# A decoder trunk's experts: gather from unsplit tokens with a twelfth weight buffer, and the second transposition behind both down products

## Chip, core and metric

The kernel runs on one core of one Trainium2 chip. The metric is the device time of one execution in microseconds; the figures of the runs are medians. Engine names: PE is TensorE (matmuls and transpositions), PEld its weight loads, DVE is VectorE, ACT is ScalarE, POOL is GpSimd, SP is SyncE, which issues the transfers.

## What is computed

A two-layer decoder trunk on 256 tokens of 1024 features, all float32. Each layer is a mixer (layer 0: pooling and sliding-window attention; layer 1: dilated attention and a gated short convolution) and a feed-forward part (layer 0: dense SwiGLU of width 2816; layer 1: eight experts of width 3584, the best two per token), each followed by a LayerNorm of the scaled residual sum. The change lies in the experts:

```
def moe_swiglu(x, w_router, w_gate, w_up, w_down):
    top_logit, top_e = lax.top_k(logits, TOP_K)          # TOP_K 2 of N_EXPERTS 8
    gates = jax.nn.softmax(top_logit, axis=-1)
    ...
        return (jax.nn.silu(xb @ w_gate[e]) * (xb @ w_up[e])) @ w_down[e]
    ...
    out = jnp.zeros((T + 1, d), jnp.float32).at[row_tok].add(y.astype(jnp.float32) * row_gate[:, None])
```

## The kernel before

**Weights.** All weights come from HBM as one long sequence of pieces, 128 partitions by 2048 float32 (1 MB), issued by SP (L191) into raw buffers as these come free. In the experts there are eleven such buffers (two opened at the start, seven in `raws`, and the tiles `xth` and `xtl` lent later). A piece is used as a sum of two single-pass fp32r halves: `W.hi` casts `wh` from the raw piece on ACT (L258), `W.lo` subtracts `wl = raw - wh` on DVE (L275) and gives the raw buffer back. There are four `wh` tiles and three `wl` tiles. `W.drop`, called when a piece has been consumed, issues the next cast and the next subtraction; all instructions stand on each engine in the order in which the Python code issues them (a manual schedule). Some pieces, called native, are not split: a float32 matmul reads the raw piece itself.

**Experts.** One unit per expert. Expert 0 and the two experts with most tokens have units of 128 token slots (heavy); the five others have 64 (light). `Experts.step` does one unit and one chunk of 512 of the 3584 columns: gate (two pieces), up (two pieces), and then the down products (two pieces) of the step before it. In a heavy unit each chunk product is three fp32r matmuls, its down pieces are native in the part where light and heavy alternate (L1224, `acc<-raw,hf`). In a light unit the high and low halves of the tokens stand side by side as 128 columns (`ml`), so a product is two matmuls (L1226 with `wh`, L1227 with `wl`) and the two halves of the result must be added afterwards: ACT copies the bank to `h` (gate L1427, up L1439), PE transposes `h` in four pieces into a bank (L1237), ACT copies one half (L1240) to `sg` (gate) or `us` (up), and DVE adds the other (L1241). Transposition and copy are `fold_of`; the add is the function that it returns. `sg * us` follows on DVE (L1466), then ACT's cast `hh` (L1467), and DVE's remainder (L1468) is left to the next step (`settle`).

**Order of steps.** Expert 0, then mostly light, light, heavy, sometimes light, heavy, and at the end seven steps of light expert 5 alone. A pair below is two light steps in a row; the first stands behind a heavy step, so the down products in it are native, and those in the second are of a light step.

**Gather.** A unit's tokens are gathered by matmuls with a one-hot matrix `oh` (L1179). The tokens were split beforehand into `xk` high and low (ACT L1089 and L1115, DVE L1091 and L1306), so a unit takes 32 fp32r matmuls of 128 rows: four parts for a heavy unit (three copied out of PSUM by ACT, one by DVE, L1185), two for a light one (both by ACT, L1190). The parts are issued between the products of other steps, one each time `part` is called.

Of the kernel before, what the change touches and what calls it, by code (L numbers as in the profile page):

```python
# [10 lines left out]
F32 = mybir.dt.float32  # L11
F32R = mybir.dt.float32r
# [75 lines left out]
def trunk(ctx, tc, stream, x_tok, x_t, pos, ln_w, ln_b, pool_bd, pool_sc, sinks, conv_w, router, cf, cb, windows,  # L88
# [20 lines left out]
    def bank():  # L109
        return rings.next("bank") if "bank" in rings.at else ps1.tile([128, 512], F32, name="bank")  # L110
# [16 lines left out]
    def split(hi, lo, src):  # L127
        nc.scalar.copy(hi, src)
        nc.vector.tensor_sub(lo, src, hi.bitcast(F32))
# [757 lines left out]
    with tc.tile_pool(name="od1", bufs=1) as e1, tc.tile_pool(name="od2", bufs=2) as e2:  # L887
# [151 lines left out]
    identb = cbf[:, B_ID:B_TRI]  # L1039
    early.close()  # L1040
    raw3 = ctx.enter_context(tc.tile_pool(name="raw3", bufs=1))
    xk, yb = [raw2.tile([128, PIECE], F32R, name=f"xk{i}") for i in range(2)], \
        raw2.tile([128, PIECE], F32R, name="yb")
    raws = [raw3.tile([128, PIECE], F32, name=f"raw{RAW1 + i}") for i in range(RAW2 + RAW3 - 3)]
    lasting = raws[:3]
    W.give_back(*raws)
    mm, na, nb, oa, ob = proj_out(wb, lambda: None)
    ctx.enter_context(tc.manual_schedule())
    xkh, xkl = [t.rearrange("p (i d) -> p i d", i=2) for t in xk]
    lgp = bank()  # L1050
    lg0 = lgp[:, :2 * NE].rearrange("p (i e) -> p i e", e=NE)

    def route(norm, c):
# [8 lines left out]
            for k in range(2):  # L1062
                nc.tensor.matmul(lg0[:, i], xt[:, k], rw[:, c + k], start=c + k == 0, stop=c + k == KC - 1)
        return logits

    def split_tokens(i):
        split(xkh[:, i], xkl[:, i], x[:, i])

    na.add(1, oa[1])
    na.finish()  # L1070
# [15 lines left out]
    W.drop(0)  # L1086
    lga()
    lga = route(na, 4)
    nc.scalar.copy(xkh[:, 0], x[:, 0])  # L1089
    lgb()  # L1090
    nc.vector.tensor_sub(xkl[:, 0], x[:, 0], xkh[:, 0].bitcast(F32))  # L1091
    lgb = route(na, 6)
    W.lo()
    mm(ob, 3, 1)
# [17 lines left out]
    lga()  # L1112
    lgb()
    keep(KEEP[2])
    nc.scalar.copy(xkh[:, 1], x[:, 1])  # L1115
    W.hi()
    W.hi()

# [42 lines left out]
    class Unit:  # L1161
# [11 lines left out]
            for i in range(2):  # L1173
                self.one_hot(self.oh[:, i], iota[:, :self.oh.shape[2]], i)

        def gather(self, a, c, b, m):
            for k in range(c, c + 512 // m):
                for i in range(2):
                    nc.tensor.matmul(b[:, (k - c) * m:(k - c + 1) * m],  # L1179
                                     (xkh, xkl)[a][:, i, k * 128:(k + 1) * 128],  # L1180
                                     self.oh[:, i], start=i == 0, stop=i == 1)

        def half(self, c, a, b, copy):
            self.gather(a, c, b, 128)
            copy(self.xg[a][:, c:c + 4], b.rearrange("p (k s) -> p k s", s=128))  # L1185

        def thin(self, a):
            b = bank()
            self.gather(a, 0, b, LIGHT)
            nc.scalar.copy(self.xg[0][:, :, a * LIGHT:(a + 1) * LIGHT], b.rearrange("p (k s) -> p k s", s=LIGHT))  # L1190

        def parts(self):
            yield self.start()
            for j in range(2 if self.light else 4):
                if self.light:
                    self.thin(j)
                else:
                    self.half(4 * (j % 2), j // 2, bank(), nc.vector.tensor_copy if j == 3 else nc.scalar.copy)
                yield

        def aim(self):
            ohb = rings.tiles["ohb"][0]
# [86 lines left out]
    nc.vector.tensor_copy(cnt, psb[:, 16:24])  # L1289
    ln2.close()  # L1290
    m2 = ctx.enter_context(tc.tile_pool(name="mo2", bufs=1, side="right"))
    rings.add("oh", [m2.tile([128, 2, 128], F32R, name="oh")])
    rings.add("ohb", [m2.tile([128, 2, 128], F32R, name="ohb")])
    rings.add("oht", [m2.tile([128, 2, 128], F32R, name="oht")])
    rings.add("h", [m2.tile([128, 512], F32, name="h")])
# [5 lines left out]
    accs = [acc() for _ in range(4)]  # L1301
    rings.add("bank", [bank() for _ in range(4)])
    places = [big_tile(t) for t in ("mh", "ml")]
    unit = Unit(places[0], 0, False, slot)
    unit.start()
    nc.vector.tensor_sub(xkl[:, 1], x[:, 1], xkh[:, 1].bitcast(F32))  # L1306
    W.lo()
    for c in (0, 4):
        unit.half(c, 0, acc(), nc.scalar.copy)
    for c in (0, 4):  # L1310
        unit.half(c, 1, bank(), nc.vector.tensor_copy if c == 0 else nc.scalar.copy)
    for _ in range(4):
        W.hi()
    W.lo()
# [4 lines left out]
    def gates():  # L1319
        nc.vector.tensor_scalar(gt[:, 0], gt[:, 1], 1.0, None, op0=OP.add)  # L1320
        nc.vector.reciprocal(gt[:, 0], gt[:, 0])
        nc.vector.tensor_mul(gt[:, 1], gt[:, 1], gt[:, 0])
        nc.vector.tensor_mul(gate, hots[0], bc(gt[:, 0]))
        nc.vector.tensor_mul(hots[1], hots[1], bc(gt[:, 1]))
        nc.vector.tensor_add(gate, gate, hots[1])
        nc.scalar.activation(x, x, AF.Copy, scale=ALPHA)

    def sort_experts():
        rank = cst[:, C_RANK:C_INV]
# [39 lines left out]
    class Experts:  # L1369
# [4 lines left out]
        def copy(self, seq, light, native):  # L1374
            o = Experts.__new__(Experts)
            o.__dict__.update(self.__dict__)
            o.units, o.y, o.seq, o.light, o.native = dict(self.units), dict(self.y), seq, light, native
            o.gather(1)
            return o
# [27 lines left out]
        def step(self, s):  # L1407
# [37 lines left out]
            if self.prev is not None:  # L1445
# [2 lines left out]
                    self.begin(pe)  # L1448
                finish(down_half(self.y[pe], pht, 0, pn, W.take(None)))
                W.drop()  # L1450
            if light:
                fold_up = fold_of(us, h)
            if left == 0:
                unit.back()
            if self.prev is not None:
                finish(down_half(self.y[pe], pht, 1, pn, W.take(None)))
                W.drop()
                if ended:
                    split_y(yb[:, :D], yb[:, D:], self.y.pop(pe))
                    ended.back()  # L1460
                    self.todo = combine_of(pe, ended.oht)
            if light:
                ht = rings.next("hh")
                s3 = sg.rearrange("p (k t) -> p k t", t=LIGHT)
                fold_up()
                nc.vector.tensor_mul(sg, sg, us)  # L1466
                nc.scalar.copy(ht[:, :, :LIGHT], s3)  # L1467
                self.late = lambda: nc.vector.tensor_sub(ht[:, :, LIGHT:], s3, ht[:, :, :LIGHT].bitcast(F32))  # L1468
                self.prev = (p, n, (ht,))
            else:  # L1470
                self.prev = (p, n, flip_h(h, (p, n, 4) in self.native))
# [35 lines left out]
    def tail(x8):  # L1507
        st = aux[:, 256:304].rearrange("p (i q s) -> p i q s", i=2, q=4)
        yh, yl = yb[:, :D], yb[:, D:]
        x8.settle()  # L1510
        spare = bank()
        for _ in range(7):
            nc.tensor.matmul(spare, xkh[:, 0, :128], xkh[:, 0, :512], start=True, stop=True)
        e, n, ht = x8.prev
        y, oht = x8.y[e], x8.units[e].oht

        def merge(c, w):
            m = slice(c, c + w)
            for i in range(2):
                b = bank()  # L1520
                nc.tensor.matmul(b[:, :w], oht[:, i], yh[:, m], start=True, stop=False)
                nc.tensor.matmul(b[:, :w], oht[:, i], yl[:, m], start=False, stop=True)
                nc.vector.scalar_tensor_tensor(x[:, i, m], b[:, :w], gate_of[:, i, e:e + 1], x[:, i, m],
                                               op0=OP.mult, op1=OP.add)
            stats(st, c, w)

        finish(down_half(y, ht, 0, n, W.take(None)))
        W.drop()
        split(yh[:, :512], yl[:, :512], y[0])
        last = down_half(y, ht, 1, n, W.take(None))  # L1530
        parts = [slice(512, 768), slice(768, D)]
        next(last)
        merge(0, 512)
        split(yh[:, parts[0]], yl[:, parts[0]], y[1][:, :256])
        next(last)
        split(yh[:, parts[1]], yl[:, parts[1]], y[2][:, :256])
        warm(AF.Sqrt, ht[0][:, 0].bitcast(F32))
        for m in parts:
            merge(m.start, 256)
        return st, wb  # L1540
# [181 lines left out]
```

## Time and profile before

| what | value |
|---|---|
| median of 3 runs | 1362.1 us (1359.48 to 1362.96) |
| profiled execution, time | 1365.56 us |
| its span, first to last instruction | 1363.8 us |
| mean granted TensorE clock | 0.990 |
| busy share PE, DVE, ACT | 97%, 80%, 67% |
| transferred | 426.61 MB, mean 313 GB/s |

The span is cut into busy and idle time of each engine. A busy share is an average over stages that have different limits, so it does not tell which engine sets the time of a stage; the order of events in the stage does. Matmul records overlap, so the time that a matmul takes is read from start to start.

### The profile page before, as it was taken

Reading aid. Unit: us, or ns where it says so; the run is one execution under the profiler, and the core shown is the slowest. Engines: PE = TensorE matmul, PEld = TensorE weight load, DVE = VectorE, ACT = ScalarE, POOL = GpSimd, SP = SyncE. Lnnn points to the kernel's source line nnn. Section 1 sums busy time; section 2 is a strip of 40 time slices with the busy share of each in tenths; the row PEclk is TensorE's granted clock in tenths of the full one; section 3 lists DMA queues with packets and bytes.
Section 4 is the critical chain, followed back from the end, with each engine's and each line's share of the span. In section 5 each row is a group of like instructions: output and inputs, shape, how many; then the busy total and the mean of one; then the engine's idle time right before and its main releaser. Section 6 shows DMA issues by size and latency. Waiting matters only on the chain. (4 is left out here: it accounts for less than half of the span.)

```text
span 1363.8 us, 18760 instructions
## 1 busy us (share of the span) xinstructions
PE 1321.2 (97%) x6944; PEld 1069.5 (78%) x6944; DVE 1084.4 (80%) x1110; ACT 917.3 (67%) x1026; POOL 2.5 (0%) x8
## 2 busy tenths in 40 slices
PE   8999999999999989999999999999999999999995
PEld 6888999988999778877777777787777877777764
DVE  6866555587655688899898899898889979988987
ACT  5735444455544477788776788778678769776883
POOL 0000000000000000000000000000000000000000
PEclk9999999999999999999999999999999999999998
DMA  8617655535424689999999999999999999999991
GB/s 261 234 62 222 205 187 186 187 124 186 155 78 149 261 307 370 346 417 401 420 387 362 377 420 420 418 419 419 419 392 419 419 405 419 420 419 350 418 411 41
DMA packets 72375, 426.61 MB, mean 313 GB/s; under 512 B 8914, under 2 KB 9682, under 8 KB 30548
## 3 DMA queue, kind: packets, MB, share of 16 engines
q1 hardware_dynamic: 71412, 424.32, 79.9%
q0 software_dynamic: 576, 0.62, 0.3%
q8 instruction: 56, 0.92, 0.3%
q10 hardware_dynamic: 288, 0.39, 0.1%
q14 instruction: 43, 0.35, 0.1%
HBM read 424.88 MB, written 1.05 MB: 312 GB/s over the span
## 5 line engine op out<-in xcount | busy, mean ns | idle before, releaser
L275 DVE TENSOR_TENSOR wl<-raw,wh 128x2048 fp32r<-128x2048 f32 (+2 forms) x435 | 823.6, 1914 | 155.6 <-ACT wh L258 126.9
L258 ACT CAST wh<-raw 128x2048 fp32r<-128x2048 f32 (+2 forms) x437 | 695.0, 1607 | 140.1 <-PE bank L318 62.8
L1226 PE MATMUL bank<-wh,ml 128*128 128x512 f32 x536 | 220.5, 411 | 1.1 <-ACT h L1427 1.1
L1227 PE MATMUL bank<-wl,ml 128*128 128x512 f32 x536 | 211.5, 395 | 0.9 <-DVE wl L275 0.6
L318 PE MATMUL bank<-wl,mh 128*128 128x512 f32 x336 | 131.8, 392 | 3.1 <-DVE wl L275 3.1
L316 PE MATMUL bank<-wh,mh 128*128 128x512 f32 x336 | 134.0, 399 | 0.0
L317 PE MATMUL bank<-wh,mh 128*128 128x512 f32 x336 | 131.4, 391 | 0.4 <-ACT mh L1185 0.4
L1227 PEld LDWEIGHTS bank<-wl,ml 128*128 128x128 f32 x536 | 100.8, 188 | 28.5 <-DVE wl L275 6.1
L1226 PEld LDWEIGHTS bank<-wh,ml 128*128 128x128 f32 x536 | 100.8, 188 | 22.6 <-issue 3.1
L316 PE MATMUL bank<-xth,wh 128*128 128x256 f32 x416 | 118.1, 284 | 0.0
L317 PE MATMUL bank<-xth,wl 128*128 128x256 f32 x416 | 117.7, 283 | 0.0
L318 PE MATMUL bank<-xtl,wh 128*128 128x256 f32 x416 | 117.7, 283 | 0.0
L1226 PE MATMUL acc<-wh,hh 128*128 128x512 f32 (+1 forms) x308 | 115.3, 381 | 0.8 <-DVE hh L1468 0.8
L1224 PE MATMUL acc<-raw,hf 128*128 128x512 f32 x256 | 115.2, 593 | 0.0
L1227 PE MATMUL acc<-wl,hh 128*128 128x512 f32 (+1 forms) x308 | 112.9, 373 | 0.0
L1224 PEld LDWEIGHTS acc<-raw,hf 128*128 128x128 f32 x256 | 47.1, 190 | 47.1 <-issue 46.0
L316 PEld LDWEIGHTS bank<-xth,wh 128*128 128x128 f32 x416 | 79.8, 192 | 0.4
L317 PEld LDWEIGHTS bank<-xth,wl 128*128 128x128 f32 x416 | 79.8, 192 | 0.4
L318 PEld LDWEIGHTS bank<-xtl,wh 128*128 128x128 f32 x416 | 79.8, 192 | 0.0
L318 PEld LDWEIGHTS bank<-wl,mh 128*128 128x128 f32 x336 | 63.5, 189 | 16.9 <-DVE wl L275 3.5
L317 PEld LDWEIGHTS bank<-wh,mh 128*128 128x128 f32 x336 | 63.5, 189 | 14.6 <-issue 1.0
L316 PEld LDWEIGHTS bank<-wh,mh 128*128 128x128 f32 x336 | 63.5, 189 | 13.8 <-issue 1.0
(284 smaller groups left out, 1849.0 us busy)
## 6 DMA issues: line engine op xcount, KB each, us to landing
raw<-in_stream SPq DMA_DIRECT2D x326, 1024.0 KB, 9.8
raw<-in_stream SPq DMA_DIRECT2D x142, 512.0 KB, 4.9
ln_wb<-in_ln_w SPq DMA_DIRECT2D x3, 512.0 KB, 8.1
ln_wb<-in_ln_b SPq DMA_DIRECT2D x3, 512.0 KB, 9.5
xraw<-in_x_t SPq DMA_DIRECT2D x4, 256.0 KB, 7.2
raw<-in_stream SPq DMA_DIRECT2D x4, 256.0 KB, 5.0
x<-in_x_tok SPq DMA_DIRECT2D x1, 1024.0 KB, 7.0
win<-in_windows SPq DMA_DIRECT2D x1, 768.0 KB, 10.9
```

The costliest lines, as they stand in the source:

```text
L258: nc.scalar.copy(self.split[k][0][:, c], self.raw[k][:, c])
L275: nc.vector.tensor_sub(wl[:, c], self.raw[k][:, c], wh[:, c].bitcast(F32))
L316: nc.tensor.matmul(o, ah, bh, start=start, stop=False)
L317: nc.tensor.matmul(o, al, bh, start=False, stop=False)
L318: nc.tensor.matmul(o, ah, bl, start=False, stop=stop)
L1224: nc.tensor.matmul(o, a if a.dtype == F32 else a.bitcast(F32), bh, start=start, stop=stop)
L1226: nc.tensor.matmul(o, a, bh, start=start, stop=False)
L1227: nc.tensor.matmul(o, a, bl, start=False, stop=stop)
```

## The change

Three edits go together. The first: the tokens stay unsplit. The gather reads the float32 tokens (`tokens`, the old `x`) with a float32 one-hot, half as many matmuls as before, and what is in PSUM is split directly by an ACT copy and a DVE subtraction: two parts for a heavy unit, one for a light unit. The outputs are summed in a new tile `xsum`, which the name `x` means from then on. The two `xk` tiles are gone. The second: `raws` has eight tiles in place of seven, so there are twelve raw buffers. The third: in a light step `fold_of(us, h)` stands behind both down products, where it stood between them. Besides, seven filler matmuls near the end (L1513) read `places[1]` in place of `xkh`.

```diff
-    xk, yb = [raw2.tile([128, PIECE], F32R, name=f"xk{i}") for i in range(2)], \
-        raw2.tile([128, PIECE], F32R, name="yb")
-    raws = [raw3.tile([128, PIECE], F32, name=f"raw{RAW1 + i}") for i in range(RAW2 + RAW3 - 3)]
+    xsum = raw2.tile([128, 2, D], F32, name="xsum")
+    yb = raw2.tile([128, PIECE], F32R, name="yb")
+    raws = [raw3.tile([128, PIECE], F32, name=f"raw{RAW1 + i}") for i in range(RAW2 + RAW3 - 2)]
...
-    nc.scalar.copy(xkh[:, 0], x[:, 0])
     lgb()
-    nc.vector.tensor_sub(xkl[:, 0], x[:, 0], xkh[:, 0].bitcast(F32))
...
-        def gather(self, a, c, b, m):
-            for k in range(c, c + 512 // m):
+        def gather(self, c, b):
+            m = LIGHT if self.light else 128
+            for k in range(512 // m):
                 for i in range(2):
-                    nc.tensor.matmul(b[:, (k - c) * m:(k - c + 1) * m],
-                                     (xkh, xkl)[a][:, i, k * 128:(k + 1) * 128],
+                    nc.tensor.matmul(b[:, k * m:(k + 1) * m], tokens[:, i, (c + k) * 128:(c + k + 1) * 128],
                                      self.oh[:, i], start=i == 0, stop=i == 1)
-
-        def half(self, c, a, b, copy):
-            self.gather(a, c, b, 128)
-            copy(self.xg[a][:, c:c + 4], b.rearrange("p (k s) -> p k s", s=128))
...
+            hi, lo = [t[:, c:c + 512 // m] for t in self.xg] if not self.light else \
+                     [self.xg[0][:, :, a * m:(a + 1) * m] for a in range(2)]
+            split(hi, lo, b.rearrange("p (k s) -> p k s", s=m))
...
-            for j in range(2 if self.light else 4):
-                if self.light:
-                    self.thin(j)
-                else:
-                    self.half(4 * (j % 2), j // 2, bank(), nc.vector.tensor_copy if j == 3 else nc.scalar.copy)
-                yield
+            for c in (0,) if self.light else (0, 4):
+                yield self.gather(c, bank())
...
-    rings.add("oh", [m2.tile([128, 2, 128], F32R, name="oh")])
+    rings.add("oh", [m2.tile([128, 2, 128], F32, name="oh")])
...
+    tokens, x = x, xsum
     unit = Unit(places[0], 0, False, slot)
     unit.start()
-    nc.vector.tensor_sub(xkl[:, 1], x[:, 1], xkh[:, 1].bitcast(F32))
     W.lo()
     for c in (0, 4):
-        unit.half(c, 0, acc(), nc.scalar.copy)
-    for c in (0, 4):
-        unit.half(c, 1, bank(), nc.vector.tensor_copy if c == 0 else nc.scalar.copy)
+        unit.gather(c, bank())
...
-        nc.scalar.activation(x, x, AF.Copy, scale=ALPHA)
+        nc.scalar.activation(x, tokens, AF.Copy, scale=ALPHA)
...
-            if light:
-                fold_up = fold_of(us, h)
             if left == 0:
                 unit.back()
             if self.prev is not None:
...
             if light:
+                fold_up = fold_of(us, h)
                 ht = rings.next("hh")
                 s3 = sg.rearrange("p (k t) -> p k t", t=LIGHT)
                 fold_up()
...
-            nc.tensor.matmul(spare, xkh[:, 0, :128], xkh[:, 0, :512], start=True, stop=True)
+            nc.tensor.matmul(spare, places[1][:, :128], places[1][:, :512], start=True, stop=True)
```

How the third edit moves instructions, on PE, in the first light step of a pair (expert 3, chunk 4; `raw` is the native down piece, `hf` the heavy step's activations, the last matmuls are the gate product of the next step). Before:

```order
L1226 MATMUL bank<-wh_82,ml 128x512
L1227 MATMUL bank<-wl_83,ml 128x512
L1224 MATMUL acc<-raw_4332,hf 128x512 x4
L1237 MATMUL bank<-cst,h 128x128 x4
L1224 MATMUL acc<-raw_4331,hf 128x512 x4
L1226 MATMUL bank<-wh_79,ml 128x512
```

and of the change:

```order
L1210 MATMUL bank<-wl_83,ml 128x512
L1207 MATMUL acc<-raw_4336,hf 128x512 x4
L1207 MATMUL acc<-raw_87,hf 128x512 x4
L1220 MATMUL bank<-cst,h 128x128 x4
L1209 MATMUL bank<-wh_79,ml 128x512
L1210 MATMUL bank<-wl_84,ml 128x512
```

The four transpositions (L1237, in the changed code L1220) now stand behind the second native down product and directly ahead of the next step's gate. On ACT in the same step, before (L1439 is the copy of `up` to `h`, L1240 the fold's copy to `us`, L258 the casts):

```order
L258 CAST wh_79<-raw_4333 128x2048
L1439 COPY h<-bank 128x512
L258 CAST wh_80<-raw_4335 128x2048
L1240 COPY us<-bank 128x256
L258 CAST wh_81<-raw_4334 128x2048
L1467 CAST hh<-sg 128x4x64
L258 CAST wh_82<-raw_4336 128x2048
```

and of the change (the same three are L1420, L1223 and L258, and `hh` is L1447):

```order
L258 CAST wh_79<-raw_88 128x2048
L1420 COPY h<-bank 128x512
L258 CAST wh_80<-raw 128x2048
L258 CAST wh_81<-raw 128x2048
L1223 COPY us<-bank 128x256
L1447 CAST hh<-sg 128x4x64
L258 CAST wh_82<-raw_4329 128x2048
L258 CAST wh_79<-raw_4330 128x2048
```

The fold's copy stands behind one more cast; on DVE the order of subtractions, the fold's add and the product is what it was. The first edit, on PE at the end of the step (1, 6), the second of a pair, where the parts for heavy unit 6 stood. Before:

```order
L1227 MATMUL acc<-wl_84,hh 128x512
L1226 MATMUL acc<-wh_82,hh 128x512
L1227 MATMUL acc<-wl_84,hh 128x512
L1226 MATMUL acc<-wh_82,hh 128x512
L1227 MATMUL acc<-wl_84,hh 128x512
L1179 MATMUL bank<-oh,xk_4328 128x128 x8
L316 MATMUL bank<-wh_79,mh 128x512
L317 MATMUL bank<-wh_79,mh 128x512
L318 MATMUL bank<-wl_85,mh 128x512
```

and of the change:

```order
L1209 MATMUL acc<-wh_82,hh 128x512
L1210 MATMUL acc<-wl_84,hh 128x512
L1209 MATMUL acc<-wh_82,hh 128x512
L1210 MATMUL acc<-wl_84,hh 128x512
L1209 MATMUL acc<-wh_82,hh 128x512
L1210 MATMUL acc<-wl_84,hh 128x512
L1220 MATMUL bank<-cst,h 128x128 x4
L316 MATMUL bank<-wh_79,mh 128x512
L317 MATMUL bank<-wh_79,mh 128x512
```

No gather part stands there now: both parts of unit 6 (L1173, eight matmuls each) are issued earlier, where the first two of the four parts stood before, and only the transposition follows the down product.

## Rows read from the trace of the kernel before

**Rows 1.** Page, busy time, share of the span and instructions of each engine.

```profile
PE 1321.2 (97%) x6944; PEld 1069.5 (78%) x6944; DVE 1084.4 (80%) x1110; ACT 917.3 (67%) x1026; POOL 2.5 (0%) x8
```

**Rows 2.** Waits: engine, its line, what it waited for: us in all, times, longest.

```profile
PEld bank L1237 <- ACT h L1439: 9.4, 13, 1.8
...
PE bank L1237 <- ACT h L1439: 3.3, 5, 1.4
```

**Rows 3.** Timeline of PE, first light step of a pair (start, us, operation).

```profile
1007.76 0.60 PE L1237 MATMUL bank<-cst,h 128*128 128x128 f32 x4
...
1011.23 0.80 PE L1226 MATMUL bank<-wh,ml 128*128 128x512 f32 x1
```

**Rows 4.** Timeline of DVE, same step up to the heavy step's successor.

```profile
1010.28 0.41 DVE L1241 TENSOR_TENSOR us<-us,bank 128x256 f32<-128x256 f32 x1
...
1011.07 2.28 DVE L275 TENSOR_TENSOR wl<-raw,wh 128x2048 fp32r<-128x2048 f32 x1
...
1035.99 8.89 DVE L275 TENSOR_TENSOR wl<-raw,wh 128x2048 fp32r<-128x2048 f32 x4
1045.50 0.42 DVE L1241 TENSOR_TENSOR sg<-sg,bank 128x256 f32<-128x256 f32 x1 [0.62 <-ACT sg L1240]
```

**Rows 5.** Timeline of ACT, the same first light step.

```profile
1008.40 0.37 ACT L1240 COPY us<-bank 128x256 f32<-128x256 f32 x1 [0.36 <-PE bank L1237]
1008.67 1.90 ACT L258 CAST wh<-raw 128x2048 fp32r<-128x2048 f32 x1
```

**Rows 6.** Timeline of PE, first light step of the next pair.

```profile
1042.41 0.39 PE L1226 MATMUL bank<-wh,ml 128*128 128x512 f32 x1
1042.73 0.50 PE L1227 MATMUL bank<-wl,ml 128*128 128x512 f32 x1
...
1044.46 0.60 PE L1237 MATMUL bank<-cst,h 128*128 128x128 f32 x4
...
1045.13 0.40 PE L1227 MATMUL bank<-wl,ml 128*128 128x512 f32 x1
...
1046.73 3.59 PE L1224 MATMUL acc<-raw,hf 128*128 128x512 f32 x8
1050.16 0.60 PE L1237 MATMUL bank<-cst,h 128*128 128x128 f32 x4
```

**Rows 7.** Stretches (window, us; busy PE, PEld, DVE, ACT, POOL; clock; DMA share; GB/s).

```profile
636.80:671.40 34.60, 34.22 (x156) 27.51 (x155) 34.40 (x25) 28.46 (x24) 0.00 (x0) 1.00 1.01 418
683.25:717.00 33.75, 30.58 (x143) 25.14 (x142) 30.64 (x26) 26.02 (x22) 0.00 (x0) 0.95 0.97 384
...
1174.40:1208.20 33.80, 33.73 (x155) 27.09 (x153) 33.61 (x21) 28.26 (x23) 0.00 (x0) 1.00 1.01 419
825.80:853.10 27.30, 27.30 (x113) 19.92 (x112) 24.36 (x17) 21.89 (x18) 0.00 (x0) 1.00 1.01 420
...
690.00:700.00 10.00, 7.89 (x38) 6.29 (x37) 8.37 (x7) 5.62 (x7) 0.00 (x0) 0.87 1.01 420
```

**Rows 8.** Timelines of PE: half a gather, and float32 matmuls of the attention.

```profile
472.48 1.95 PE L1179 MATMUL bank<-oh,xk 128*128 128x128 f32 x16
...
429.11 2.57 PE L1013 MATMUL bank<-v,pt 128*128 128x64 f32 x22
```

**Rows 9.** Timelines of PE where a gather part or a transposition waits.

```profile
695.35 1.11 PE L1179 MATMUL bank<-oh,xk 128*128 128x128 f32 x8 [2.11 <-ACT h L1439]
...
1264.17 0.66 PE L1237 MATMUL bank<-cst,h 128*128 128x128 f32 x4 [1.02 <-ACT h L1439]
```

**Rows 10.** Timeline of DVE ahead of the first expert.

```profile
473.57 0.69 DVE L1185 CAST mh<-bank 128x512 fp32r<-128x512 f32 x1 [0.67 <-PE bank L1179]
```

**Rows 11.** Page, DMA issues (count, KB each, median us from issue to landing).

```profile
raw<-in_stream SPq DMA_DIRECT2D x326, 1024.0 KB, 9.8
```

**Rows 12.** Waits in the stretch from 0 to 400 us.

```profile
ACT wh L258 <- DMA raw<-in_stream: 20.8, 22, 2.3
```

**Rows 13.** Waits in the stretch from 560 to 1210 us, of SP's queue.

```profile
SPq L191 <- DVE wl L275: 318.6, 156, 4.8
```

## Prediction before the run

> **What bounds the kernel now.** I read the busy time first. PE is busy 97% of the span, DVE 80%, ACT 67% [rows 1], which would make PE the bound and leave DVE a fifth of the span in reserve. The waits show what PE still loses around the moved transposition: behind the copy of `up` to `h` the second fold's matmuls and weight loads idle for 3.3 and 9.4 us [rows 2]; since the load idle partly lies beside running matmuls, I put PE's own loss at about 6. An average hides stages, so I read the stretches next. Nine of them begin at the `us` add of the first light step of a pair, and end with the last subtraction before the first fold of the next pair. In the first of the nine DVE is busy 34.40 of 34.60 us, in the last 33.61 of 33.80 [rows 7]: it has 0.2 us of idle time in a whole stretch. A tenth pair, from 683.25, has 3.1 idle. Where one light step alternates with one heavy step, DVE is busy 24.36 of 27.30 [rows 7], so it has 2.9 in hand there.
>
> Whether that full DVE sets the time is told by the end of a stretch. There four subtractions run from 1035.99 to 1044.88 [rows 4], and the first matmul that needs the last of them starts at 1045.13 [rows 6]: 0.25 us later. One piece earlier PE already has a gap: 1042.41 to 1042.73 is 0.32 us [rows 6], while the seven from there to 1044.46 take 0.25 each. So PE and DVE are level there. Whatever delays DVE at the start of a stretch by more than some 0.2 us arrives at PE.
>
> **The fold's move, native down products.** Before, PE transposes at 1007.76, between the two native down products [rows 3]. ACT's copy runs at 1008.40 [rows 5], and DVE adds at 1010.28 without having waited, since until then it subtracts [rows 4]; so the fold is hidden. In the change the second down product comes first. It takes what the first one takes in the next pair, 1046.73 to 1050.16, 3.43 us [rows 6], so the transposition starts at 1011.19. From a transposition to the add of a waiting DVE it is 1044.46 to 1045.50, 1.04 us [rows 4, 6]. The add then starts at 1012.23 and not at 1010.28, 1.95 us later. The cast that ACT now does first, 1.90 us [rows 5], starts as early as its piece is there and ends before PE has transposed, so it adds nothing; if it were late, at most its 1.90 would come on top.
>
> Queued behind the waiting add on DVE are the product `sg * us`, the subtraction at 1011.07 and every other one of the stretch [rows 4]. Less the 0.2 that it had idle, 1.75 us arrives at PE per pair: 9 x 1.75 = **+15.8 us**. Lower bound: DVE has up to 0.4 more idle where PE and DVE are not quite level (0.25 and 0.2 together), 1.5 x 9 = 13.5; upper bound: no idle helps and the tenth pair pays too, 10 x 1.95 = 19.5. Next on ACT: `hh` and the casts behind the copy are late by as much, but ACT is busy 28.26 of 33.80 us [rows 7] and catches up. SP's next pieces are issued 1.75 later; a piece lands 9.8 us after its issue [rows 11], and no cast waits for a piece from 560 us on, so this is hidden.
>
> **The fold's move, fp32r down products.** In the second step of a pair the second down product is eight fp32r matmuls, at most 0.25 us each by the seven above, 2.0 in all, so the transposition is 2.0 later; the chain of DVE reaches that add 1.75 later anyway, and before the add there lay behind its subtractions as well. 0; the tenths that could come of it are in the upper bound. In lone light steps DVE's 2.9 covers 1.95: 0. In the last seven steps one wait of 1.02 us for the same copy ended at 1264.17 [rows 9]; behind the down products that copy is done: **-1.0** (0 if DVE is late there).
>
> **The gather.** A half unit is 16 matmul records in 1.95 us, 0.122 each; the float32 matmuls of the attention, also short, take 22 records in 2.57 us, 0.117 each, two records to a matmul [rows 8]. So 16 float32 matmuls of 32 records take what 32 fp32r ones took: PE 0. What bounds it is two-sided: if a record of 128 columns took up to twice one of 64, 8 units x 3.9 = +31 (the fp32r row with 128 columns, at the same 0.122, speaks against that); if it were one record, -16. I take 0. By the Trainium skill, FP8 and Floating Point Precision, TensorE Precision Notes, true FP32 takes four passes through the array; by passes alone 16 matmuls would cost 64 passes where 32 stood. That is the third rival, below.
>
> DVE gets one more half-size subtraction per unit, 0.69 us [rows 10], and ACT one copy less. Two light units (4 and 5) are gathered inside two of the nine stretches: 2 x 0.6 = **+1.2**, none (0) if PE had lead there. Ahead of expert 0 two subtractions of the tokens go and two of half the width come, one of them nearer to the first product: 0, between -1.2 and +1.4 (twice 0.69).
>
> Unit 6's third part stood behind the copy of `up` in step (1, 6): PE waited 2.11 us for it [rows 9], and the granted clock, at its upper level (2.4 GHz) before, fell to a mean of 0.87 over that stretch [rows 7], 1.3 us more. No part stands there in the change, since two parts do. At most 3.4 comes back; DVE is idle only 10.00 less 8.37, 1.63 us, in those 10 us [rows 7]. Between 1.6 and 3.4 I take **-2.5**.
>
> **The twelfth buffer.** SP's queue waits 318.6 us in 560 to 1210 for a subtraction to free a buffer [rows 13], so with twelve each piece is issued one piece earlier. It is worth that only if somebody waits for pieces: the 20.8 us that ACT does all lie before 400 us [rows 12], ahead of the place where the buffer is opened. DMA runs at 418 to 420 GB/s in the stretches [rows 7], so 1 MB takes 2.5 us and eleven buffers are 27 us of stream, against 9.8 to land: **0**. The Trainium skill, Perfetto Trace Analysis, Optimization Strategy, says that a gap repeating on the engine that should be full can mean too few buffers for the next tile. PE's repeated gap here ends with a copy of `h` and not with a transfer [rows 2]; by that rule the second rival below would come true.
>
> The seven fillers near the end read another tile of the same shape: 0.
>
> **Sum.** 15.8 - 1.0 + 1.2 - 2.5 = +13.5. The profiled execution takes 1365.56 us (span 1363.8 and 1.76 around it), 3.5 above the median; against its own time that is 1379.1, against the median of 1362.1 it is **1375.6**. The forecast's own range: 13.5 - 1.0 - 3.4 - 1.2 = +7.9 to 19.5 + 1.2 + 1.4 - 1.6 = +20.5, so 1370 to 1383.
>
> **Rivals.**
> *PE-bound, faster.* If DVE's subtractions have lead that the records hide, say by an earlier start through the twelfth buffer, the later add costs nothing, and PE regains the 6 us behind `h` and 3.4 at unit 6: 1362.1 - 9.4 = 1352.7. It decides where DVE's spare time per pair passes 1.95 us. For it: 97% and 80% [rows 1]. Against it: 0.2 us idle of 34, and matmuls level with subtractions [rows 4, 6, 7]. 0.09.
> *Pieces bound, faster.* The stream is full at 420 GB/s, and the buffer could even it out. If all of 9.4 + 3.3 = 12.7 of the gaps [rows 2] hung on that: 1362.1 - 12.7 = 1349.4. Against it: no cast waits for a piece there. 0.03.
> *Passes, slower.* By four passes an eight-unit gather would add 8 x 16 x 2 x 0.122 = 31 us to the sum, less where it falls on PE's waits: about 1375.6 + 31 = 1407. Against it is the price of the float32 records [rows 8]. 0.03.
> *Every light step behind a heavy one pays.* Sixteen light steps stand behind a heavy one; if the lone ones pay as well, 16 x 1.95 = 31.2 - 2.5 = 28.7: 1391. Against it: DVE's 2.9 idle there. 0.05.
> *No change.* PE's regained waits (9.4) and DVE's losses could cancel, if only some of the nine stretches are level, as few as five (8.8): 1361.5. For it: I measured the level at one end and idle time at the others. 0.09.
>
> **Numbers.** The forecast holds 0.71. Slower by over 0.3% (4.1 us, about what a measurement of this kernel tells from no change): 0.71 + 0.03 + 0.05 = 0.79; same 0.09; faster 0.09 + 0.03 = 0.12. The range holds the forecast's own and reaches down to no change: 1361 to 1383; left out are the two fast rivals and the two dear ones, 0.20.
>
> **What would show it.** Right: in the changed profile DVE's `us` add of a pair's first step has an idle of 1 to 2 us before it, ended by ACT's copy to `us`, and the matmuls of the subtracted halves (the line of `wl`) wait for DVE by some 1.7 us in each of nine pairs, in sum over 10 us; the period from one pair to the next grows by 1.7; the clock stays at its upper level at 690 to 700; the gather's records are 0.11 to 0.12 us apart, 32 for a unit. Wrong: the adds wait, but PE's matmuls don't (the first rival); the casts or SP's order moved the pieces; gather records 0.2 us apart; or waits of PE at folds that have not gone although the fold moved.

## The result, and the profile after

The changed kernel takes 1376.58 us (median of 6 runs, 1370.24 to 1378.7), the kernel before 1361.95 (6 runs). The ratio is 1.0096, with a 95% interval of 1.0073 to 1.012: slower by 14.6 us by the medians, where 13.5 was forecast. The profiled execution took 1372.3 us (span 1370.5), 4.3 below its median, as the one of before lay 3.6 above its own; so stages are compared below, and not the two spans.

Busy time on the page, as [rows 1]:

```profile
PE 1326.8 (97%) x6944; PEld 1065.6 (78%) x6944; DVE 1084.7 (79%) x1116; ACT 907.2 (66%) x1016; POOL 2.5 (0%) x8
```

The shares have hardly moved, and tell nothing. PE has the same 6944 records, so the gather with half as many matmuls keeps its count. DVE has six instructions more, ACT ten fewer.

DVE's timeline in the first light step of the pair that [rows 4] showed (start, us, operation, idle before and what ended it):

```profile
1006.01 4.57 DVE L275 TENSOR_TENSOR wl<-raw,wh 128x2048 fp32r<-128x2048 f32 x2 [2.27 <-ACT wh L258]
1012.47 0.42 DVE L1224 TENSOR_TENSOR us<-us,bank 128x256 f32<-128x256 f32 x1 [1.89 <-ACT us L1223]
...
1013.27 2.29 DVE L275 TENSOR_TENSOR wl<-raw,wh 128x2048 fp32r<-128x2048 f32 x1
```

The add, which did not wait before, now waits 1.89 us for ACT's copy, and the subtraction behind it starts 0.80 us after it, as it did. ACT and PE in the same step, to be held against [rows 5] and [rows 3]; ACT first:

```profile
1006.36 3.70 ACT L258 CAST wh<-raw 128x2048 fp32r<-128x2048 f32 x2
1012.07 0.37 ACT L1223 COPY us<-bank 128x256 f32<-128x256 f32 x1 [2.01 <-PE bank L1220]
```

and PE, to the first light step of the pair after it:

```profile
1011.43 0.60 PE L1220 MATMUL bank<-cst,h 128*128 128x128 f32 x4
1011.79 0.48 PE L1209 MATMUL bank<-wh,ml 128*128 128x512 f32 x1
...
1041.99 0.39 PE L1209 MATMUL bank<-wh,ml 128*128 128x512 f32 x1
1042.48 0.50 PE L1210 MATMUL bank<-wl,ml 128*128 128x512 f32 x1
...
1044.21 0.39 PE L1209 MATMUL bank<-wh,ml 128*128 128x512 f32 x1
1044.68 0.50 PE L1210 MATMUL bank<-wl,ml 128*128 128x512 f32 x1
...
1055.92 0.48 PE L1209 MATMUL bank<-wh,ml 128*128 128x512 f32 x1
```

ACT has both casts done by 1010.06, then waits 2.01 us for the transposition, so the extra cast in front costs nothing here. PE goes from the transposition straight on, and pays later: at 1042.48 and 1044.68 a matmul with `wl` starts 0.49 and 0.47 us after its `wh` partner, where 0.23 is usual. From 1011.79 to 1055.92 is 44.13 us. Before, the same stretch began at 1011.23 [rows 3] and ended with this row of PE's timeline:

```profile
1053.63 0.80 PE L1226 MATMUL bank<-wh,ml 128*128 128x512 f32 x1
```

That is 42.40 us, so the pair is 1.73 us longer. The waits of the stretch from 560 to 1210 us say who is waited for:

```profile
DVE us L1224 <- ACT us L1223: 22.3, 12, 1.9
...
PE acc L1210 <- DVE wl L275: 4.0, 11, 0.4
...
PE bank L1210 <- DVE wl L275: 2.3, 4, 0.7
...
PEld bank L1210 <- DVE wl L275: 14.5, 32, 1.2
PEld acc L1210 <- DVE wl L275: 9.6, 13, 0.8
```

Of the kernel before, the same stretch has this row of weight loads that wait for subtractions:

```profile
PEld bank L1227 <- DVE wl L275: 5.7, 13, 0.7
```

The add's row is new. PE waits for subtractions in 15 matmuls, in sum 6.3 us; the weight loads of such matmuls wait 24.1 us where it was 5.7, part of it beside running matmuls. Two stretches, as in [rows 7]: the 10 us in which unit 6's third part had stalled PE (that step begins 2.0 us earlier in the changed kernel, so the place of the stall still lies inside), and from an add to the end of the chain that it heads:

```profile
690.00:700.00 10.00, 9.76 (x44) 7.48 (x43) 9.96 (x11) 7.75 (x8) 0.00 (x0) 1.00 0.97 384
...
1012.47:1046.90 34.43, 33.43 (x152) 26.23 (x151) 34.21 (x22) 27.90 (x23) 0.00 (x0) 1.00 1.01 421
```

In the pair DVE is still busy all but 0.2 us, and now it is PE that idles, by 1.0 us. At unit 6 the stall is gone: PE is busy 9.76 us where it was 7.89, at the upper level of the clock.

### The profile page after: what moved, and what is told of

The parts are those of the page before. It is cut to its first block, busy times and chain, and to the rows that moved or that the text cites. A ratio compares the mean times of both kernels' runs of the same rounds, so it can differ in the third digit from the quotient of the medians.

```text
span 1370.5 us, 18731 instructions
## 1 busy us (share of the span) xinstructions
PE 1326.8 (97%) x6944; PEld 1065.6 (78%) x6944; DVE 1084.7 (79%) x1116; ACT 907.2 (66%) x1016; POOL 2.5 (0%) x8
## 4 chain that ended last, share of the span: by engine, by line
PE 76%; DVE 11%; DMA 6%; ACT 4%; issue 3%; SPq 0%; DVEq 0%; ACTq 0%
PE bank L318 9%; PE bank L317 9%; PE bank L316 9%; PE acc L1207 7%; DVE wl L275 7%; PE bank L1210 6%; PE bank L1209 6%; DMA raw<-in_stream 6%; PE acc L318 4%; PE acc L316 4%; PE acc L317 4%; PE acc L1210 3%; PE acc L1209 3%; ACT wh L258 2%; PE bank L1173 2%
## 5 line engine op out<-in xcount | busy, mean ns | idle before, releaser
L258 ACT CAST wh<-raw 128x2048 fp32r<-128x2048 f32 (+2 forms) x437 | 689.0, 1606 | 128.3 <-PE bank L318 62.0
L1210 PEld LDWEIGHTS bank<-wl,ml 128*128 128x128 f32 x536 | 100.7, 188 | 37.0 <-DVE wl L275 16.5
L1207 PE MATMUL acc<-raw,hf 128*128 128x512 f32 x256 | 112.4, 592 | 0.0
L1210 PEld LDWEIGHTS acc<-wl,hh 128*128 128x128 f32 x308 | 58.0, 188 | 20.1 <-DVE wl L275 9.8
L317 PEld LDWEIGHTS bank<-wh,mh 128*128 128x128 f32 x336 | 63.6, 189 | 12.6
```

The costliest lines, as they stand in the source:

```text
L258: nc.scalar.copy(self.split[k][0][:, c], self.raw[k][:, c])
L317: nc.tensor.matmul(o, al, bh, start=False, stop=False)
L1207: nc.tensor.matmul(o, a if a.dtype == F32 else a.bitcast(F32), bh, start=start, stop=stop)
L1210: nc.tensor.matmul(o, a, bl, start=False, stop=stop)
```

## The experiments

Each ratio is to the kernel before, timed beside that run (medians of 1361.95 to 1363.12). The table gives two more times, of one profiled execution each, read from PE's timeline, from the first gate matmul of one step to that of another: two neighbouring pairs (from step (2, 2) to (6, 4); 768.36 to 853.15 before), and the experts from step (0, 1) to the end of the span. A step is named by its expert and chunk. The second time leaves out what lies ahead of the experts, and step (0, 0).

| kernel | median us | ratio (95%) | two pairs | experts |
|---|---|---|---|---|
| before | 1361.95 | | 84.79 | 877.19 |
| the change | 1376.58 | 1.0096 (1.0073 to 1.012) | 88.25 | 889.63 |
| 1: fold behind, alone | 1378.79 | 1.0104 (1.0086 to 1.0123) | 88.23 | 891.65 |
| 2: gather and buffer alone | 1360.71 | 0.9984 (0.9969 to 1.0) | 84.83 | 874.91 |
| 3: the change, 11 buffers | 1376.23 | 1.0105 (1.0088 to 1.0123) | 88.28 | 889.65 |
| 4: the change, add deferred | 1373.32 | 1.0075 (1.0058 to 1.0091) | 87.66 | 888.78 |
| 5: fold behind native products | 1376.88 | 1.0106 (1.0088 to 1.0123) | 88.28 | 891.93 |
| 6: fold behind fp32r products | 1361.78 | 0.9983 (0.9971 to 0.9995) | 84.83 | 875.57 |
| 7: deferred in two stages | 1362.95 | 1.0009 (0.9995 to 1.0023) | 85.89 | 878.67 |
| 8: remainder on POOL | 1379.13 | 1.0121 (1.0104 to 1.0138) | 89.12 | 894.93 |
| 9: the parts that paid | 1358.37 | 0.9983 (0.9965 to 1.0001) | 84.84 | 874.71 |
| 10: ACT's copy deferred too | 1360.52 | 0.9984 (0.9971 to 0.9997) | 85.18 | 875.56 |

### 1: the fold's move alone

```diff
-            if light:
-                fold_up = fold_of(us, h)
             if left == 0:
...
             if light:
+                fold_up = fold_of(us, h)
                 ht = rings.next("hh")
```

This is the third edit on the kernel before, nothing else.

> The kernel before with the third edit alone: the fold of up stands behind both down products, the gather and the eleven buffers are as before. Theory (the later add delays DVE's full chain): nine pairs of light steps are 1.7 us longer each, so 15.5 us, less 1.0 at expert 5: about 1362 + 14.5 = 1376, with DVE's add waiting 1.9 us for ACT's copy in the first step of each pair. Rival A (the time comes from the native gather or the buffer): no change, 1362. Rival B (PE-bound, the fold's waits come back): 1353 to 1358.

It took 1378.79 us, and the two pairs 3.44 more than before, 1.72 each. DVE's timeline has the wait of the changed kernel:

```profile
1015.27 4.58 DVE L275 TENSOR_TENSOR wl<-raw,wh 128x2048 fp32r<-128x2048 f32 x2 [2.27 <-ACT wh L258]
1021.72 0.42 DVE L1241 TENSOR_TENSOR us<-us,bank 128x256 f32<-128x256 f32 x1 [1.88 <-ACT us L1240]
```

Rivals A and B fall. From step (0, 1) on the experts are 14.46 us longer; 14.5 was expected. By the medians it is 16.5 (1362.27 beside it); in its profile 2.0 more lie in step (0, 0), for which see the end of the section on the prediction. Over the nine stretches of the prediction the loss is 14.8 us, 1.35 to 1.75 in each; the tenth pair loses nothing.

### 2: the gather and the buffer alone

The changed kernel with `fold_up = fold_of(us, h)` back between the two down products, as the diff of run 1 read upwards.

> The changed kernel with the fold of up put back between the two down products: native gather and twelfth buffer alone. Theory: the pairs have their old period, the stall at unit 6's third part stays away and the way to expert 0 is some 2 us shorter: 1355 to 1360. Rival A (native gather or buffer cost the time): 1376. Rival C (the two edits are worth nothing by themselves): 1362.

1360.71 us; the pairs are as before, and the experts 2.28 us shorter. The interval ends at 1.0, so the gain is small and not far from nothing, yet no cost. Runs 1 and 2 add up: 14.46 - 2.28 = 12.18, and the change has 12.44. Inside the 2.28 lie losses too. Steps (1, 5) and (1, 6), with unit 6, are 3.69 us shorter (38.52 to 34.83), but step (2, 0), two steps on, is 1.24 longer: PE waits there, 0.70 us at one place, for DVE's subtraction of the finished unit's output:

```profile
718.34 0.50 PE L1267 MATMUL bank<-yb,oht 128*128 128x512 f32 x1 [0.70 <-DVE yb L129]
```

A row of the stretches shows why DVE is late:

```profile
684.00:718.00 34.00, 32.59 (x157) 26.50 (x155) 33.93 (x29) 28.56 (x27) 0.00 (x0) 1.00 1.00 399
```

DVE is busy 33.93 of 34 us, where it had 3.1 us idle in about the same place before [rows 7, the stretch from 683.25]. Its work is not more: one instruction of 0.7 us for the gather lies there in either kernel. PE, no longer stalled, has run into the full DVE, and from (1, 5) to the end of (2, 0) 2.56 us are left of the gain. Unit 7's steps, (3, 3) and (7, 0), are 0.7 shorter. The steps around the gather of unit 2, (1, 1) and (1, 2), are 1.1 longer, with DVE busy 15.89 of the 16 us from 592 to 608; those around unit 3, (6, 1) and (2, 1), are 0.2 longer. Step (0, 0), outside the count, is 0.4 longer here (12.73 against 12.34), as in every profile with the new gather.

### 3: eleven buffers

```diff
-    raws = [raw3.tile([128, PIECE], F32, name=f"raw{RAW1 + i}") for i in range(RAW2 + RAW3 - 2)]
+    raws = [raw3.tile([128, PIECE], F32, name=f"raw{RAW1 + i}") for i in range(RAW2 + RAW3 - 3)]
```

> The changed kernel with seven tiles in raws, so eleven raw buffers in place of twelve. Theory (pieces land long before they are cast): as the changed kernel, 1376 within 2 us. Rival (the twelfth buffer gives some of the time back): slower, up to 12 us. Rival (the earlier transfers cost something): faster than 1372.

1376.23 against 1376.58, and the experts 889.65 us against 889.63: the twelfth buffer is worth nothing here.

### 4: the add deferred to the next step

```diff
-                fold_up()
-                nc.vector.tensor_mul(sg, sg, us)
-                nc.scalar.copy(ht[:, :, :LIGHT], s3)
-                self.late = lambda: nc.vector.tensor_sub(ht[:, :, LIGHT:], s3, ht[:, :, :LIGHT].bitcast(F32))
+                def late():
+                    fold_up()
+                    nc.vector.tensor_mul(sg, sg, us)
+                    nc.scalar.copy(ht[:, :, :LIGHT], s3)
+                    nc.vector.tensor_sub(ht[:, :, LIGHT:], s3, ht[:, :, :LIGHT].bitcast(F32))
+                self.late = late
```

> The changed kernel with the fold behind both down products, but the add to us, the product, the cast hh and its remainder are issued after the first gate piece of the next step, so that DVE subtracts one more piece before it needs the transposed half. Theory (only the waiting add at the head of DVE's queue costs): the 1.7 us per pair go, 1358 to 1363. Rival (the later copy on ACT and the casts behind it cost as much): 1370 to 1377.

A miss: 1373.32 us, and 1.43 of the 1.73 us per pair stay ((87.66 - 84.79) / 2). DVE's timeline, in the same pair:

```profile
1015.34 0.42 DVE L1224 TENSOR_TENSOR us<-us,bank 128x256 f32<-128x256 f32 x1
...
1017.21 0.43 DVE L1450 TENSOR_TENSOR hh<-sg,hh 128x256 fp32r<-128x256 f32 x1 [0.99 <-ACT hh L1449]
...
1032.71 0.42 DVE L1450 TENSOR_TENSOR hh<-sg,hh 128x256 fp32r<-128x256 f32 x1 [0.47 <-ACT hh L1449]
```

The add no longer waits, but the remainder of `hh`, which now follows the product at once, does: in both steps of the pair, together 1.46 us, since it needs ACT's cast `hh`, which in the first step stands behind a cast of a piece besides. One wait at the head of DVE's queue has taken the place of another. The time is in the range of the rival, and the theory as it was put, that only the waiting add costs, did not hold; whether the rest is ACT or DVE this run can't tell. Run 7 can.

### 5 and 6: the fold behind one kind of down product

Run 5 moves the fold of the kernel before only in light steps whose down products are native, run 6 only in the others.

```diff
+            behind = self.prev is not None and (self.prev[0], self.prev[1], 5) in self.native
-            if light:
+            if light and not behind:
                 fold_up = fold_of(us, h)
...
             if light:
+                if behind:
+                    fold_up = fold_of(us, h)
                 ht = rings.next("hh")
```

In run 6 `behind` is the negation.

> The kernel before with the fold of up moved behind both down products only in light steps whose down products are native (16 steps, the first of every pair among them). Theory: the cost lies in the first step of a pair, so all of it is here: about 1.7 us for each of nine pairs, 1362 + 15.5 = 1377.5. Rival (the second step's fold, behind fp32r products, has a share): 1365 to 1372.

> The counterpart: the kernel before with the fold of up moved only in light steps whose down products are fp32r. Theory: DVE reaches that add later than PE has transposed in either order, so nothing in the pairs, 1.1 us less at expert 5 and 0.8 more at the end: 1362 within 1.5. Rival (it has a share): over 1364.

1376.88 and 1361.78 us: all of the cost is in the native steps, 3.49 us in the two pairs, and the other steps cost nothing there (84.83 against 84.79). Over the experts run 6 even gains 1.62 us, and its interval lies below 1; 1.31 of that lie in steps (1, 5) and (1, 6), where unit 6's gather stalls PE and for which the expectation had nothing.

### 7: deferred in two stages

```diff
+                def late():
+                    fold_up()
+                    nc.vector.tensor_mul(sg, sg, us)
+                    nc.scalar.copy(ht[:, :, :LIGHT], s3)
+
+                def later():
+                    nc.vector.tensor_sub(ht[:, :, LIGHT:], s3, ht[:, :, :LIGHT].bitcast(F32))
+                self.late = [late, later]
...
-            if self.late is not None:
-                self.late()
-                self.late = None
+            if self.late:
+                self.late.pop(0)()
```

The four lines of the changed kernel that run 4 replaced are gone here too, and the tail calls `settle` twice.

> The changed kernel with the add to us, the product and the cast hh issued after the first gate piece of the next step, as in the run before, and the remainder of hh on DVE one piece later still, so that DVE waits neither for ACT's copy nor for ACT's cast. Theory (DVE's waits at the head of its queue are the cost, and the run with one stage only changed a wait of 1.9 us into waits of 1.0 and 0.5): the period of the pairs of the kernel before comes back, 1358 to 1363. Rival (the pieces' subtractions are late for another reason, such as the later transposition itself): 1370 to 1376.

1362.95 us, the level of before; the fold still stands behind both down products. (That level includes what the gather gains: against run 2 the experts are 3.8 us longer.) DVE's timeline of such a step, and then ACT's:

```profile
1008.57 0.42 DVE L1224 TENSOR_TENSOR us<-us,bank 128x256 f32<-128x256 f32 x1
...
1010.15 2.29 DVE L275 TENSOR_TENSOR wl<-raw,wh 128x2048 fp32r<-128x2048 f32 x1 [0.70 <-ACT wh L258]
1012.36 0.42 DVE L1451 TENSOR_TENSOR hh<-sg,hh 128x256 fp32r<-128x256 f32 x1
```

```profile
1007.93 0.37 ACT L1223 COPY us<-bank 128x256 f32<-128x256 f32 x1 [2.01 <-PE bank L1220]
1008.20 1.92 ACT L258 CAST wh<-raw 128x2048 fp32r<-128x2048 f32 x1
```

Neither the add nor the remainder waits. Of the 1.73 us per pair 0.55 is left, and what DVE waits for now is ACT's cast of the next piece, 0.70 us: on ACT that cast stands behind the copy to `us`, which waits 2.01 us for the late transposition.

### 8: one DVE instruction on POOL

```diff
-                self.late = lambda: nc.vector.tensor_sub(ht[:, :, LIGHT:], s3, ht[:, :, :LIGHT].bitcast(F32))
+                self.late = lambda: nc.gpsimd.tensor_sub(ht[:, :, LIGHT:], s3, ht[:, :, :LIGHT].bitcast(F32))
```

> The changed kernel with one DVE instruction per light step, the remainder of hh (0.42 us), on POOL. Theory (DVE's chain sets the pairs): two such instructions lie in each chain, 0.84 us less of 1.7 in nine pairs: 1376.5 - 7.6 = 1369. Rival (the time is set by something else): 1376. Rival (POOL is slow, or slows DVE at memory): 1380 or more.

1379.13 us, the pairs 0.44 us longer than in the change instead of 0.84 shorter each. POOL's timeline, and then DVE's, beside it and later:

```profile
1017.05 2.23 POOL L1448 TENSOR_TENSOR hh<-sg,hh 128x256 fp32r<-128x256 f32 x1 [33.13 <-PE bank L1210]
```

```profile
1016.39 7.24 DVE L275 TENSOR_TENSOR wl<-raw,wh 128x2048 fp32r<-128x2048 f32 x3
...
1041.50 6.68 DVE L275 TENSOR_TENSOR wl<-raw,wh 128x2048 fp32r<-128x2048 f32 x3
```

The remainder takes 2.23 us on POOL (spans on POOL are rough), where DVE took 0.42, and the three subtractions beside it take 7.24 us, where three with nothing beside them take 6.68. So DVE got rid of 0.42 (0.33 from start to start) and lost 0.56. POOL by itself is not that slow. The last remainder of all, with DVE idle beside it:

```profile
1353.61 0.72 POOL L1448 TENSOR_TENSOR hh<-sg,hh 128x256 fp32r<-128x256 f32 x1 [14.13 <-POOLq L1590]
```

This one takes 0.72 us, and one at 983.18, with DVE busy only for part of it, 0.74; the other 33, with DVE busy beside them, take 1.5 to 2.6. So each slows the other. That is the mechanism of the third expectation, though the time fell 0.9 us short of its range; the time follows DVE's chain in this direction too. The last step is 1.9 us longer than in the change: PE waits 2.19 us for the remainder there, and from 1355 to 1358 us the granted clock is at its lower level (1.2 GHz, 0.50), where the change's end shows 1.00.

### 9: the parts that paid

Run 2, with the fold behind the fp32r products only, and between the down products in the last step (`behind` is `left > 0` and not native).

> The parts that paid, together: native gather and twelfth buffer, the fold of up behind both down products only where these are fp32r, and between them in the last step of all. Theory (the two gains, 1.6 and 1.3 us, lie in different places, and without the last step the second is some 0.8 more): 1358 to 1360, below both kernels. Rival (one gain contains the other): 1361.

1358.37 us, the lowest median of all, 3.7 below the runs of before beside it (1362.07), but the interval, 0.9965 to 1.0001, takes in no change. The profile speaks for the rival: the experts took 874.71 us, against 874.91 in run 2. The two gains lie in the same place: from (1, 5) to the end of (2, 0) run 6 is 1.32 us shorter than before, run 2 2.56, and this run 2.23. Nor did the last step get its 0.8 back, though its own fold stands between the down products again. DVE's timeline has the reason in the step before it:

```profile
1316.52 0.42 DVE L1224 TENSOR_TENSOR us<-us,bank 128x256 f32<-128x256 f32 x1 [0.75 <-ACT us L1223]
```

That add waits 0.75 us where it did not wait before, and from there DVE works without a wait up to the last step's `us` add, so the delay reaches the end. The time is clearly below the change, and not shown to be below the kernel before.

### 10: ACT's copy deferred too

```diff
-                fold_up = fold_of(us, h)
+                copy_up = fold_of(us, h, True)
...
-                    fold_up()
+                    copy_up()()
```

On run 7; with the new argument `fold_of` issues the transposition only, and ACT's copy when it is called.

> The changed kernel, deferred in two stages as before, and ACT's copy of the transposed half now also behind the next step's first cast, so that neither DVE nor a cast waits for the transposition. Theory (of 1.7 us per pair some 1.2 were the add at the head of DVE's queue and some 0.5 the cast behind the copy on ACT): the pairs come back to the period of before, nine times 0.5 us less than the run with two stages, 1358 to 1360. Rival (the 0.5 is something else): 1362 to 1364.

1360.52 us (interval 0.9971 to 0.9997), the pairs 85.18, so 0.2 us per pair is left of the 1.73. ACT's and DVE's timelines, the add without a wait:

```profile
1009.55 0.38 ACT L1225 COPY us<-bank 128x256 f32<-128x256 f32 x1 [0.20 <-PE bank L1220]
```

```profile
1010.20 0.42 DVE L1226 TENSOR_TENSOR us<-us,bank 128x256 f32<-128x256 f32 x1
```

With the transposition behind both down products all the same, the loss is all but gone: it was not the place of the transposition on PE, but what waits for it at the head of the queues of DVE and ACT. (As in run 7, the time includes the gain of the gather; the experts take 0.65 us more than in run 2.)

## Why the prediction was right

**The fold behind native products: right, to a tenth.** The transposition was to start at 1011.19 and the add at 1012.23; they started at 1011.43 and 1012.47, the step itself having begun 0.19 later (that the two profiles are so close there is chance; the differences are what counts). A pair was to lose 1.75 us and lost 1.73, and runs 5 and 6 place it in the native steps. All nine were to cost 15.8 and cost 14.8 alone (run 1). One sign came out smaller: the matmuls with `wl` wait 6.3 us in sum, not over 10; the rest shows in their weight loads. That DVE sets the end of the pairs is shown from three sides: taking its wait away (7 and 10) brings most of the time back, loading it more (8) costs more, and PE's matmuls with `wl` wait at the end of the chain.

**The extra cast on ACT: right for the change, too short as a reason.** The text had ACT catch up, since it is idle for 5.5 us in a stretch. In the change the copy's lateness hides behind DVE's own. Once DVE's wait is gone, 0.55 per pair stays, with DVE waiting for the cast behind the copy (run 7); when the copy moves too, 0.2 stays (run 10). Idle time elsewhere in a stretch does not help a queue whose head waits.

**The fold behind fp32r products, and lone light steps: right but for the end.** Nothing in the pairs (run 6), nothing in lone light steps, though the adds wait there just as long. The lone step (2, 5) in the changed kernel, DVE's timeline:

```profile
851.91 0.42 DVE L1224 TENSOR_TENSOR us<-us,bank 128x256 f32<-128x256 f32 x1 [1.88 <-ACT us L1223]
```

In the change (6, 4), behind it, is 0.32 us shorter and (2, 6) 0.32 longer. Of the 12 adds that wait in the stretch, nine head the chains of pairs and cost time, and three stand in lone steps and cost none: the same wait is paid or not by what DVE has in hand behind it, as the text had it. The 1.0 us at expert 5 came back (1.1 in step (5, 1)), but the last step of all became 0.8 longer, where the text had nothing: the add of the step before it waits 0.75 us, and DVE has nothing in hand up to the end (run 9).

**The gather on PE: right.** The start of the experts in the changed kernel, PE's timeline:

```profile
464.60 3.81 PE L1173 MATMUL bank<-oh,x 128*128 128x128 f32 x32 [0.69 <-DVE oh L1162]
```

These are 16 float32 matmuls in 32 records, 0.119 us each, where 16 records of the old gather took 1.95 [rows 8]. The rival by passes falls; for this shape the trace disagrees with what was worked out from the four passes of the Trainium skill, FP8 and Floating Point Precision, TensorE Precision Notes: two records at the old record's time, so 32 records for 32, not twice the time. That goes for 128 columns only: at 512 the native down products take 3.43 us for eight records [rows 6], four matmuls of 0.86 us each, about three and a half times the 0.23 to 0.25 of an fp32r one.

**The gather's other terms: unit 6 right, the others not.** Unit 6 was to give 2.5, between what DVE's idle time and PE's stall allow, and gave 2.56: the two steps with the stall became 3.7 us shorter, and DVE, full, took 1.1 of that back within the next two (run 2). Units 4 and 5 were to cost 0.6 each inside full stretches; the steps around them came out even, within 0.2 us. What the text had at nothing came out otherwise: unit 2 cost 1.1, unit 3 0.2 and step (0, 0) 0.4, and unit 7's steps gave 0.7. Together -1.3 had been forecast for the gather, and -2.28 + 0.39, so -1.9, is what run 2's profile shows; that the sum is so near is in part luck, since the misses cancel. It sits inside what a measurement can tell from nothing.

**The twelfth buffer: right,** by run 3. The repeated gap on PE that the Trainium skill, Perfetto Trace Analysis, Optimization Strategy, would let one blame on too few buffers was not one of buffers here. With twelve buffers and the old place of the fold (run 2) the second fold's matmuls and weight loads idle behind the copy of `up` as before, 3.9 and 10.4 us in the span where it was 3.3 and 9.4 [rows 2]:

```profile
PEld bank L1220 <- ACT h L1420: 10.4, 14, 1.5
```

What the sum does not explain is the part ahead of the experts. In the profiles the change has 12.4 us more in the experts and 0.4 in step (0, 0), 12.8 in all; the medians differ by 14.6, and where the other 1.8 lie isn't shown. The first product of expert 0 starts between 467.5 and 474.3 us in the twelve profiles, early and late both with the old gather (469.8 to 474.3) and with the new (467.5 to 473.7). In the profiles of runs 1 and 5 step (0, 0) took 2.0 us more than before: TensorE's clock stood at its lower level (1.2 GHz, 0.50 in the rows) for 6.8 us around the start of expert 0. Row of the stretches, run 1:

```profile
471.60:478.40 6.80, 6.80 (x24) 5.91 (x23) 4.32 (x5) 4.36 (x6) 0.00 (x0) 0.50 0.39 145
```

PE had waited 0.69 us for the one-hot matrix ahead of it, at 468.5, but it waits as long in the changed kernel, whose clock stays up there. The kernel before and run 10 have the lower level a little earlier, for 3.4 us, ahead of the first product. What starts this stays open. It is one reason why single spans here differ by more than the edits.

## To carry over

Before an instruction is moved to a later place on one engine, look at which instruction of another engine's in-order queue will wait for it, and at what stands behind that one; a queue that is full for a whole stretch pays the wait almost in full (1.73 of 1.95 us here), whatever its busy share of the span says, and one with time in hand behind it pays nothing. If the move is wanted for other reasons, move the consumers on every engine as well, the remainder behind them included, so that no queue meets the late result at its head. Test an edit of several parts in its parts: here one cost 14 us, one gained about 2, and one did nothing. And where a stall is removed, look two steps on: the engine that it had kept waiting may become the next limit.

## What was not expected of the hardware

POOL took 2.23 us for a subtraction of 128 x 256 elements that DVE does in 0.42, and while it ran, three DVE subtractions took 7.24 us instead of 6.68; with DVE idle the same subtraction took 0.72 us on POOL. The granted clock was at its lower level (0.50) for 6.8 us at the start of expert 0 in two of ten experiments, and not in the others, at the price of 2 us. A float32 matmul of 128 columns took twice the time of an fp32r one (two records of 0.119 us against one of 0.122), one of 512 columns some three and a half times (0.86 against 0.23 to 0.25).
